# A hybrid decoder layer on one core: first norm from x loaded transposed, conditioning loads in order

## The chip, the cores and the metric

One core of a Trainium2 chip runs the whole program in one launch. The metric is the device time in microseconds (us), the median of three runs. Engines: TensorE (PE, its weight loads PEld), VectorE (DVE), ScalarE (ACT), GpSimd (POOL) and SyncE (SP), which issues most DMAs.

## The reference, cut to what matters

One step of a decoder layer over 1024 prompt rows and 8 sample rows, D_MODEL = 1024, float32. Only the beginning matters here:

```
mod = silu(c) @ w_ada + b_ada
shift1, scale1, gate1, shift2, scale2, gate2 = split(mod, 6)
h = RMSNorm(x) * (1 + scale1) + shift1
proj = h @ w_in      # conformer GLU | q, k, v | z | beta | decay | merge gates A, B
...
```

The prompt rows share one c, each of the 8 sample rows has its own. Behind proj come a Conformer branch (GLU, depthwise convolution of width 31, LayerNorm, swish, a projection), a gated DeltaNet branch (short convolution of width 4 and SiLU on q, k and v, a chunked gated delta rule with a triangular solve per chunk, a norm, a projection), the merge of the two, and a feed-forward part with its own norm; then a final norm.

## The kernel before, in words

T = 1032 columns are the 1024 + 8 rows of x. Feature-major tiles hold 128 of the 1024 features each: u[k] and the pair h_hi[k], h_lo[k], k = 0 to 7, all 128 x 1032. Products of full precision are three passes: h and each weight are split into a rounded part and the rest (h_hi and h_lo, whi and wlo), and a product is whi with h_hi, whi with h_lo, wlo with h_hi, over 344 columns each (a third of T), added up in a PSUM bank over k: 24 matmuls per bank. These are the "main products" of this text (`mm` in the profile).

hybrid() does not issue instructions. It records operations with the tiles that they read and write, and the class Plan (lines 135 to 475) orders them: a list scheduler that steps through a modelled time, keeps one queue per engine, and on each engine takes the ready operation with the lowest `plan.prio` (ties go in recorded order). Durations come from Plan.cost; tiles come out of rings with limits per class (caps: 34 slots of 4 KB and 21 of 2 KB a partition, eight PSUM banks). What it found is then emitted, so every instruction has the line of that one loop, L475, and goes by its tile's name. A change of one priority, size or dependency can thus reorder all engines, until the plans meet again.

The head of the program:
- SP loads constants, c transposed, then eight pieces of w_ada (`wk`, 256 KB each: piece q = 0) and x in nine blocks of 128 rows (`xin`, the last with the 8 sample rows). ADAQ (line 30) holds the priorities of the four conditioning pieces' loads, FIRST those of the first weights.
- Norm of x (loop at line 588): per block ACT squares and sums along the row (`ss`), POOL takes the power -1/2 (`rs`), DVE scales the rows (`xn`), TensorE transposes them (`xT`, eight 128 x 128 matmuls), ACT and DVE copy them out of PSUM into u.
- Conditioning (ada_first, line 609, called for q = 0 to 3): 32 matmuls of `wk` with cT into the bank `ada`, a copy `mo`, the transpose `adaT`, and on DVE the shift, scale and s1 = norm weight * (1 + scale) of two feature tiles.
- Per piece, for its two tiles k = 2q and 2q + 1 (line 670): DVE u[k] = u[k] * s1 + shift; ACT casts it to h_hi[k]; h_lo[k] = u[k] - h_hi[k], on DVE for even k and on POOL for odd.
- `ba`: beta and decay logits straight from u, 64 one-pass matmuls in all; from them cum (sums of the decay along a chunk), its transpose cumT, a store to DRAM (scrG) and loads of it spread over partitions (`glb`, `Gb`), which edec and Dm need.

Main products go on in an order that the plan finds: GLU columns for the Conformer (conformer, line 1113), q, k, v of one head after the other. For a head, DVE runs the short convolution (`qkvq`: one scaling and three sums of 1024 columns), ACT the SiLU, TensorE transposes (`tT`) and products of k and q (`kq`); DVE makes Dm, Am and drives the solve, half a head at a time, with small TensorE steps `i` and `j` between (32 x 32 blocks; i16, i32, j32, j64 below), then TensorE steps through the scan (`pw`, `po`, `py`, `pd`).

```
plan.prio = ADAQ[q]
wk = tl("wk", [128, 512], "wk")
SP.dma_start(wk, I["w_ada"][q, k])
...
V.tensor_scalar(uk, uk, s1[:, f, 0:1], shift[:, f, 0:1], op0=ALU.mult, op1=ALU.add)
copy(Hh[k], u[k], ("ACT",))
sub(Hl[k], u[k], f32(Hh[k]), ("DVE", "POOL")[k % 2:k % 2 + 1])
```

Of the kernel before, what the change touches and what calls it, by code (L numbers as in the profile page):

```python
# [10 lines left out]
ALU = mybir.AluOpType  # L11
# [18 lines left out]
ADAQ = (-1, 0.2, 0.4, 0.5)  # L30
# [456 lines left out]
def hybrid(tc, I, O):  # L487
    nc = tc.nc
    with ExitStack() as ctx:
        ctx.enter_context(tc.manual_schedule())  # L490

        def pool(name, space=None, st=ctx, **k):
# [14 lines left out]
            acc=("P4", 10), cs=("P4", 2), ff=("PS", 8), ada=("P4", 2),  # L507
# [71 lines left out]
        def evac_T(src, dst, i, n, cls):  # L579
            for hf in range(2):  # L580
                pb = bank(cls, "xT")
                with plan.group("PE"):
                    for k in range(4):
                        kk = 4 * hf + k
                        TE.transpose(pb[:, k * 128:k * 128 + n], src[0:n, kk * 128:(kk + 1) * 128], ident[0:n, 0:n])
                dst(hf, pb)

        for i in range(9):
            n = 128 if i < 8 else 8
            cs = slice(i * 128, i * 128 + n)  # L590
            xt = tl("xin", [128, 1024], "xin")
            SP.dma_start(xt[0:n], I["x"][i * 128:i * 128 + n])
            xn = tl("xin", [128, 1024], "xn")
            ss, rs = tl("s8", [128, 1], "ss"), tl("s8", [128, 1], "rs")
# [4 lines left out]
            def norm_T(hf, pb):  # L599
                if i == 8:  # L600
                    copy(xs[:, 4 * hf:4 * hf + 4, :], pb.rearrange("p (k c) -> p k c", c=128)[:, :, 0:8])
                    return
                pairs = [(u[4 * hf + k][:, cs], pb[:, k * 128:k * 128 + n]) for k in range(4)]
                plan.any_of({e: [(m, p, {}) for p in pairs] for e, m in (("ACT", "copy"), ("DVE", "tensor_copy"))})
            evac_T(xn, norm_T, i, n, "x")
# [3 lines left out]
        def ada_first(q):  # L609
            ps = bank("s", "ada")  # L610
            for k in range(8):
                plan.prio = ADAQ[q]
                wk = tl("wk", [128, 512], "wk")
                SP.dma_start(wk, I["w_ada"][q, k])
                wk_op[0] = plan.last
                plan.prio = -1
                if k == 0:
                    plan.touch = (ps,)
                with plan.group("PE"):
                    for j in range(4):  # L620
                        TE.matmul(ps[32 * j:32 * j + 32, 0:128], lhsT=cT[:, k, :], rhs=wk[:, j * 128:j * 128 + 128],
                                  start=(k == 0), stop=(k == 7), tile_position=(0, 32 * j))
                plan.prio = 0
# [46 lines left out]
        for q in range(4):  # L670
# [1080 lines left out]
def arrange(a):  # L1751
# [6 lines left out]
    def cols(v, n):  # L1758
# [8 lines left out]
        x=x, xT=x.T.reshape(8, 128, T).transpose(1, 0, 2), cT=c.T.reshape(8, 128, 9).transpose(1, 0, 2),  # L1767
# [59 lines left out]
```

## Time and profile before

| | us |
|---|---|
| median of three runs | 1897.24 |
| lowest, highest | 1893.27, 1898.88 |
| the profiled execution | 1896.7 |
| its span in the trace | 1895.0 |
| TensorE busy in the span | 1819.3 (96 %) |
| DVE, POOL, ACT busy | 1436.5, 856.7, 847.1 |

The profile is one execution. Times in it count from the start of the span; the profiled execution lasted 1.7 us longer than the span. The granted clock of TensorE has a mean of 0.987 of full speed over it. Idle time of TensorE, and time at a lower clock, is what the kernel can still lose; idle time of the other engines costs nothing by itself.

### The profile page before, as it was taken

What the parts mean: (1) busy time and instruction counts of PE and PEld (TensorE: products, weight loads), DVE (VectorE), ACT (ScalarE), POOL (GpSimd) and SP (SyncE); (2) the same over time, 40 slices, a digit from 0 to 9 for tenths busy, and PEclk for the clock granted to TensorE, in tenths of its full rate; (3) what the DMA queues carried; (4) which work ended last, traced back from release to release, by engine and by line L of the source; (5) the groups of instructions that cost most, each with busy time, mean ns of one, the idle gap of its engine ahead of it and who ended that gap; (6) DMA issues with size and microseconds to landing.
All of it is one profiled execution on the core that took longest, in us unless ns stands there. A gap on an engine that the chain in (4) does not pass through costs nothing. (4 is left out here: it accounts for less than half of the span.)

```text
span 1895.0 us, 41996 instructions
## 1 busy us (share of the span) xinstructions
PE 1819.3 (96%) x16205; PEld 1742.7 (92%) x16205; DVE 1436.5 (76%) x3137; ACT 847.1 (45%) x2089; POOL 856.7 (45%) x734
## 2 busy tenths in 40 slices
PE   7998999999998999999999999899999999999995
PEld 5988999989897888999999989899999999999995
DVE  6576778668788999998191767975565578999997
ACT  5444445444454545421240125555555565433344
POOL 3354445444445432543222145332322338888864
PEclk9999999999999999999999999899999999999998
DMA  9321111212122477942444754344454484553433
GB/s 344 69 73 57 65 36 41 69 35 75 60 79 75 144 248 259 341 151 80 144 164 140 226 181 165 99 146 135 138 163 132 138 265 163 167 181 126 133 124 90
DMA packets 164188, 261.46 MB, mean 138 GB/s; under 512 B 27252, under 2 KB 90876, under 8 KB 163972
## 3 DMA queue, kind: packets, MB, share of 16 engines
q1 hardware_dynamic: 158228, 241.91, 39.6%
q10 hardware_dynamic: 5760, 16.88, 2.3%
q8 instruction: 127, 2.08, 0.5%
q14 instruction: 73, 0.60, 0.1%
HBM read 189.76 MB, written 69.64 MB: 137 GB/s over the span
## 5 line engine op out<-in xcount | busy, mean ns | idle before, releaser
L475 PE MATMUL mm<-h_hi,whi 128*128 128x344 f32 x1344 | 462.0, 344 | 0.0
L475 PE MATMUL mm<-h_hi,wlo 128*128 128x344 f32 x1344 | 432.1, 321 | 3.4 <-POOL rawq L475 3.4
L475 PE MATMUL mm<-h_lo,whi 128*128 128x344 f32 x1344 | 431.6, 321 | 0.0
L475 POOL TENSOR_TENSOR wlo<-raw,whi 128x512 fp32r<-128x512 f32 x168 | 250.5, 1504 | 347.8 <-ACT whi L475 280.3
L475 PE MATMUL ff<-fbh,wp 128*128 128x258 f32 x1808 | 330.1, 283 | 3.8 <-DVE accu L475 1.7
L475 PE MATMUL ff<-bp,wp 128*128 128x258 f32 x2688 | 324.5, 283 | 1.6 <-DVE bp L475 0.9
L475 PEld LDWEIGHTS ff<-bp,wp 128*128 128x128 f32 x2688 | 323.4, 189 | 2.5 <-DVE bp L475 1.3
L475 PEld LDWEIGHTS ff<-fbh,wp 128*128 128x128 f32 x1808 | 280.5, 189 | 7.5 <-DVE accu L475 3.0
L475 PEld LDWEIGHTS mm<-h_hi,whi 128*128 128x128 f32 x1344 | 255.1, 190 | 11.4 <-issue 5.4
L475 PEld LDWEIGHTS mm<-h_hi,wlo 128*128 128x128 f32 x1344 | 254.6, 189 | 3.7 <-POOL rawq L475 3.7
L475 PE MATMUL ff<-fbl,wp 128*128 128x258 f32 x904 | 255.5, 283 | 1.7 <-DVE fbl L475 1.7
L475 PEld LDWEIGHTS mm<-h_lo,whi 128*128 128x128 f32 x1344 | 255.6, 190 | 0.0
L475 POOL TENSOR_TENSOR wp<-raw,wp 128x512 fp32r<-128x512 f32 x93 | 141.6, 1528 | 199.8 <-ACT wp L475 179.2
L475 DVE SCALAR_TENSOR_TENSOR av<-gl,vecs,av 128x1024 f32<-128x1024 f32 x120 | 181.7, 1514 | 1.9
L475 PEld LDWEIGHTS ff<-fbl,wp 128*128 128x128 f32 x904 | 170.8, 189 | 2.2 <-DVE fbl L475 2.2
L475 POOL TENSOR_TENSOR fbl<-fbl,fbh 128x516 fp32r<-128x516 f32 x100 | 149.4, 1528 | 9.8 <-issue 7.7
L475 ACT CAST wp<-raw 128x512 fp32r<-128x512 f32 x159 | 95.8, 615 | 128.6 <-DVE raw L475 54.7
L475 DVE TENSOR_TENSOR ft<-ff,ft 128x258 f32<-128x258 f32 x160 | 67.3, 422 | 92.6 <-PE ff L475 91.6
L475 ACT CAST whi<-raw 128x512 fp32r<-128x512 f32 x168 | 99.1, 619 | 79.7 <-DMA raw<-w_gdn_out 32.6
L475 ACT ACTIVATE ft<-ft 128x258 f32<-128x258 f32 x224 | 93.2, 419 | 70.9 <-DVE ft L475 66.9
L475 POOL TENSOR_TENSOR wp<-s,wp 128x512 fp32r<-128x512 f32 x31 | 53.3, 1721 | 85.3 <-ACT wp L475 85.3
L475 ACT ACTIVATE gt<-mm 128x344 f32<-128x344 f32 x72 | 32.1, 457 | 112.9 <-PE mm L475 88.1
(398 smaller groups left out, 3641.1 us busy)
## 6 DMA issues: line engine op xcount, KB each, us to landing
raw<-w_ff SPq DMA_DIRECT2D x128, 256.0 KB, 4.3
fD<-ft SPq DMA_DIRECT2D x228, 129.0 KB, 3.0
fbl<-fD SPq DMA_DIRECT2D x57, 516.0 KB, 3.5
raw<-w_in SPq DMA_DIRECT2D x112, 256.0 KB, 4.3
wk<-w_ada SPq DMA_DIRECT2D x32, 512.0 KB, 4.8
wk<-w_ada SPq DMA_DIRECT2D x32, 256.0 KB, 5.3
raw<-w_o SPq DMA_DIRECT2D x32, 256.0 KB, 4.2
sp_z<-gt ACTq DMA_DIRECT2D x8, 516.0 KB, 5.4
```

The source lines that it names most:

```text
L475: getattr(h, m)(*[x.real() if isinstance(x, Ref) else x for x in a], **{q: x.real() if isinstance(x, Ref) else x for q, x in k.items()})
```

## The change

x is no longer loaded by rows. Its transpose (made on the host already, as an input of the kernel before) is loaded straight into u[k], eight loads of 516 KB, and the 8 sample columns once more into xs. ACT squares each u[k] (1032 columns), DVE adds the squares of k = 0 to 6 up, and 18 matmuls with a single column of ones sum the two tiles (the sum and the square of k = 7) over the partitions: `ss`, nine columns. One power on POOL (128 x 9) gives rs. Two DVE products spread rs on diagonals (`dg`, four blocks of 128 x 128 each), and eight matmuls with ones make of them two PSUM banks (`rB`) that hold each prompt column's factor in all partitions; a small one does the same for the samples.

Per tile, u = u * s1 * rB is now two DVE operations of 512 columns with a bank as an operand; ACT adds the shift while it casts to h_hi (1024 columns, and 8 apart); DVE alone makes h_lo = (u + shift) - h_hi (1024, and 8 apart); ACT adds the shift to u itself, for ba.

The conditioning loads: ADAQ's first value goes from -1 to 0.05, so x is loaded ahead of w_ada. Piece 0 and the first half of piece 2 stay loads of 256 KB in the 2 KB ring; pieces 1 and 3 and the second half of piece 2 are loads of 512 KB (class wk4, up to ten slots of the 4 KB ring). TensorE's ada matmuls come in groups of 16. The Conformer's weights wait until the last conditioning load has been issued.

```diff
-ADAQ = (-1, 0.2, 0.4, 0.5)
+ADAQ = (0.05, 0.2, 0.4, 0.5)
...
-        for i in range(9):
-            n = 128 if i < 8 else 8
...
-            SP.dma_start(xt[0:n], I["x"][i * 128:i * 128 + n])
...
-            A.activation(xn[0:n], xt[0:n], AF.Square, accum_out=ss[0:n])
-            V.tensor_scalar(ss[0:n], ss[0:n], 1.0 / D, EPS, op0=ALU.mult, op1=ALU.add)
-            P.tensor_tensor(rs[0:n], ss[0:n], mhalf[0:n, 0:1], ALU.pow)
-            V.tensor_scalar(xn[0:n], xt[0:n], rs[0:n], None, op0=ALU.mult)
...
-            evac_T(xn, norm_T, i, n, "x")
+        SP.dma_start(xs, I["xT"][:, :, S:T])
+        for k in range(8):
+            SP.dma_start(u[k], I["xT"][:, k])
+            sq = tl("xin", [128, T], "sq")
+            A.activation(sq, u[k], AF.Square)
+            if k == 0:
+                sqs = sq
+            elif k < 7:
+                V.tensor_tensor(sqs, sqs, sq, ALU.add)
+        pss = bank("x", "ss")
+        with plan.group("PE"):
+            for j in range(9):
+                n = 128 if j < 8 else 8
+                for i, t in enumerate((sqs, sq)):
+                    TE.matmul(pss[0:n, j:j + 1], lhsT=t[:, j * 128:j * 128 + n], rhs=ones[:, 0:1], start=i == 0, stop=i == 1)
...
+        P.tensor_tensor(rs, ss, mhalf[:, 0:1].to_broadcast([128, 9]), ALU.pow)
...
+        for i in range(2):
+            dg = tl("xin", [128, 4, 128], "dg")
+            V.tensor_tensor(dg, ident.unsqueeze(1).to_broadcast([128, 4, 128]),
+                            rs[:, 4 * i:4 * i + 4].unsqueeze(2).to_broadcast([128, 4, 128]), ALU.mult)
+            pb = bank("x", "rB1")
+            with plan.group("PE"):
+                for j in range(4):
+                    TE.matmul(pb[:, j * 128:j * 128 + 128], lhsT=ones, rhs=dg[:, j], start=True, stop=True)
+            rB1.append(pb)
...
+                if q % 2 or (q, k4) == (2, 1):
+                    two = [tl("wk4", [128, 2, 512], "wk") for _ in range(2)]
...
+                        SP.dma_start(t, I["w_ada"][q, k:k + 2].rearrange("k p n -> p k n"))
+                else:
+                    wk = [tl("wk", [128, 512], "wk") for _ in range(4)]
...
-                uk = u[k][:, 0:S]
-                V.tensor_scalar(uk, uk, s1[:, f, 0:1], shift[:, f, 0:1], op0=ALU.mult, op1=ALU.add)
-                copy(Hh[k], u[k], ("ACT",))
-                sub(Hl[k], u[k], f32(Hh[k]), ("DVE", "POOL")[k % 2:k % 2 + 1])
+                for i in range(2):
+                    ui = u[k][:, 512 * i:512 * i + 512]
+                    V.scalar_tensor_tensor(ui, ui, s1[:, f, 0:1], rB1[i], op0=ALU.mult, op1=ALU.mult)
+                uk, us = u[k][:, 0:S], u[k][:, S:T]
+                A.copy(Hh[k][:, S:T], us)
+                A.activation(Hh[k][:, 0:S], uk, AF.Identity, bias=shift[:, f, 0:1])
+                V.tensor_tensor(Hl[k][:, S:T], us, f32(Hh[k][:, S:T]), ALU.subtract)
+                V.scalar_tensor_tensor(Hl[k][:, 0:S], uk, shift[:, f, 0:1], f32(Hh[k][:, 0:S]), op0=ALU.add, op1=ALU.subtract)
+                A.activation(uk, uk, AF.Identity, bias=shift[:, f, 0:1])
...
-            hi, lo = wload(w_in[OFF["ug"] + i], 8, (sg,))
+            hi, lo = wload(w_in[OFF["ug"] + i], 8, (sg,), after=(wk_op[0],))
...
-            hi, lo = wload(w_in[OFF["u"] + i], 8, (gl,))
+            hi, lo = wload(w_in[OFF["u"] + i], 8, (gl,), after=(wk_op[0],))
```

Since the plan is made anew, the order of the instructions changes on every engine. From TensorE's second conditioning round in mid-program on (about 750 us in the trace before; TensorE's last 8392 of 13992 matmuls) the lists are the same again, on the other engines from about half of theirs on. What moves before that is shown at three places, out of the two programs' lists of instructions (output<-inputs, shape, how many alike in a row).

The first is TensorE from its first instruction. Before, up to the second `adaT`:

```order
L475 MATMUL ada<-wk,cT 32x128 x32
L475 MATMUL adaT<-con,mo 128x128
L475 MATMUL xT<-con,xn 128x128 x48
L475 MATMUL ada<-wk,cT 32x128 x8
L475 MATMUL xT<-con,xn 128x128 x4
L475 MATMUL ada<-wk,cT 32x128 x4
L475 MATMUL xT<-con,xn 128x128 x4
...
```

And after, up to its first main product (`rB` are the two banks of factors):

```order
L475 MATMUL ss<-ones,sq 128x1 x16
L475 MATMUL ss<-ones,sq 8x1 x2
L475 MATMUL ada<-wk,cT 32x128 x32
L475 MATMUL adaT<-con,mo 128x128
L475 MATMUL rB<-dg,ones 128x128 x4
L475 MATMUL rB<-dg,ones 128x128 x4
L475 MATMUL ada<-wk,cT 32x128 x16
L475 MATMUL rB1s<-dgs,ones 128x8
L475 MATMUL ada<-wk,cT 32x128 x16
L475 MATMUL adaT<-con,mo 128x128
L475 MATMUL mm<-h_hi,whi 128x344
```

The 72 transposes are gone; 64 ada matmuls stand ahead of the first main product, and 64 behind it. Before, 84 stand ahead and 44 behind.

The second is DVE around the first head's q convolution (`st` are small sums for the norms of q and k, `glu` the Conformer's). Before, from the copy of cum on:

```order
L475 COPY gc<-cum 128x72
L475 COPY gTs<-cumT 72x128
L475 TENSOR_SCALAR egn<-egn 128x72
L475 TENSOR_TENSOR edec<-glb,gc 128x72
L475 TENSOR_SCALAR Dm<-Gb,gc 128x128 x4
L475 SCALAR_TENSOR_TENSOR glu<-sg,mm 128x344 x3
L475 TENSOR_TENSOR ktok<-tT,edec 128x512 x2
L475 TENSOR_SCALAR qkvq<-rawq,vecs 128x1024
L475 TENSOR_SCALAR st<-st 128x4
L475 SCALAR_TENSOR_TENSOR qkvq<-rawq,vecs,qkvq 128x1024
```

After, from the same copy:

```order
L475 COPY gc<-cum 128x72
L475 TENSOR_SCALAR egn<-egn 128x72
L475 COPY gTs<-cumT 72x128
L475 TENSOR_SCALAR qkvq<-rawq,vecs 128x1024
L475 TENSOR_SCALAR st<-st 128x4
L475 SCALAR_TENSOR_TENSOR qkvq<-rawq,vecs,qkvq 128x1024 x2
L475 TENSOR_TENSOR edec<-glb,gc 128x72
L475 SCALAR_TENSOR_TENSOR glu<-sg,mm 128x344
L475 TENSOR_TENSOR st<-st 128x4
L475 TENSOR_TENSOR ktok<-tT,edec 128x512
...
L475 SCALAR_TENSOR_TENSOR qkvq<-rawq,vecs,qkvq 128x1024
```

Two of qkvq's three sums have moved ahead of edec; the third stands behind it, behind Dm and both ktok. On TensorE the transposes of qkvq stand behind 291 main products after, and behind 351 before.

The third is TensorE in the solve of the second half-head (numbers of the tiles kept). Before, the last i step and the j step:

```order
L475 MATMUL i32_2210<-T32_2048,Pt_2182 32x32 x16
L475 MATMUL j32_2249<-Tt2_2242,Am_1878 32x32 x8
```

After, the same two and what stands between them:

```order
L475 MATMUL i32_1811<-T32_1676,Pt_1796 32x32 x16
L475 MATMUL mm_1830<-h_hi0_334,whi_1768 128x344
L475 MATMUL mm_1830<-h_lo0_359,whi_1768 128x344
L475 MATMUL mm_1830<-h_hi0_334,wlo_1769 128x344
L475 MATMUL pw_1834<-Sn_1809,qkvk_706 128x128
L475 MATMUL po_1836<-Sn_1809,Gb_931 128x128
...
L475 MATMUL tT_1846<-con_74,qkvv_1281 128x128 x4
...
L475 MATMUL py_1862<-R_1844,U0_78 128x128
L475 MATMUL j32_1864<-Tt2_1853,Am_1538 32x32 x8
```

Where two steps followed each other, nine main products and small ones now stand between them; from the first i step of this half-head to its j step there are 33 main products and products of the scan after, and nine before.

## Rows read from the trace of the kernel before

**Rows 1.** The page, its parts 1 and 2: busy time, share and instructions of each engine; and TensorE's busy tenths in 40 equal slices of the span.

```profile
PE 1819.3 (96%) x16205; PEld 1742.7 (92%) x16205; DVE 1436.5 (76%) x3137; ACT 847.1 (45%) x2089; POOL 856.7 (45%) x734
...
PE   7998999999998999999999999899999999999995
```

**Rows 2.** Windows of TensorE after the head: stretch, its length, busy time (instructions), granted clock, DMA share, GB/s.

```profile
60.00:100.00 40.00, 40.00 (x259) 1.00 0.46 110
100.00:200.00 100.00, 89.22 (x882) 0.93 0.16 55
200.00:400.00 200.00, 198.55 (x2074) 1.00 0.16 52
400.00:750.00 350.00, 338.62 (x4031) 0.99 0.35 120
```

**Rows 3.** TensorE's timeline: start, duration, operation, and in brackets the idle time before it and what released it.

```profile
102.05 1.09 PE L475 MATMUL tT<-con,qkvq 128*128 128x128 f32 x8 [0.88 <-ACT qkvq L475]
...
116.53 0.32 PE L475 MATMUL mm<-h_lo,whi 128*128 128x344 f32 x1
120.25 0.66 PE L475 MATMUL mm<-h_hi,wlo 128*128 128x344 f32 x1 [3.40 <-POOL rawq L475]
...
174.12 0.45 PE L475 MATMUL i<-T,Pt 32*32 32x32 f32 x32
...
179.76 0.64 PE L475 MATMUL j<-Tt,Am 32*32 32x32 f32 x16 [5.19 <-DVE Tt L475]
```

**Rows 4.** Windows of TensorE where the granted clock (the column behind the busy time) falls, and the one ahead of the first.

```profile
21.00:24.00 3.00, 1.00 (x8) 0.95 1.07 397
24.00:27.00 3.00, 3.00 (x21) 0.50 1.04 379
120.00:126.00 6.00, 5.75 (x21) 0.50 0.00 0
180.00:184.00 4.00, 4.00 (x43) 0.50 0.37 82
```

**Rows 5.** Windows of all engines in the head: length, busy time of PE, PEld, DVE, ACT, POOL, then granted clock, DMA share, GB/s.

```profile
0.00:15.00 15.00, 5.74 (x66) 1.92 (x67) 2.71 (x15) 4.52 (x8) 2.10 (x12) 1.00 0.86 303
15.00:20.00 5.00, 5.00 (x23) 4.67 (x24) 3.81 (x13) 4.69 (x15) 1.66 (x3) 1.00 1.03 409
...
35.00:46.00 11.00, 10.48 (x133) 7.59 (x128) 9.10 (x11) 3.42 (x6) 7.97 (x8) 1.00 1.05 394
```

**Rows 6.** SP's queue of DMA issues: start, time over which the loads are issued, how many.

```profile
33.82 3.90 SPq L475 DMA_DIRECT2D wk<-w_ada  x6
```

**Rows 7.** DMA issues between 36 and 37.6 us: how many, KB each, median us from issue to landing.

```profile
wk<-w_ada SPq DMA_DIRECT2D x2, 256.0 KB, 6.1
```

**Rows 8.** TensorE's timeline at its first main products.

```profile
33.71 0.42 PE L475 MATMUL ada<-wk,cT 128*32 128x128 f32 x8
...
35.15 0.42 PE L475 MATMUL mm<-h_hi,whi 128*128 128x344 f32 x1
```

**Rows 9.** A window of TensorE alone: busy time and instructions from the first main product to 60 us.

```profile
35.00:60.00 25.00, 24.48 (x249) 1.00 0.49 183
```

**Rows 10.** POOL's timeline: its first h_lo and its last.

```profile
34.97 2.48 POOL L475 TENSOR_TENSOR h_lo<-u,h_hi 128x1032 fp32r<-128x1032 f32 x1 [2.00 <-ACT h_hi L475]
...
54.48 2.50 POOL L475 TENSOR_TENSOR h_lo<-u,h_hi 128x1032 fp32r<-128x1032 f32 x1 [2.00 <-ACT h_hi L475]
```

**Rows 11.** Groups of instructions of the first 60 us: engine, operation, shapes, count, then busy us and mean ns of one, then idle time before them and its releasers.

```profile
L475 PE MATMUL xT<-con,xn 128*128 128x128 f32 x64 | 12.5, 365 | 4.6 <-DVE ss L475 2.5 <-DVE xn L475 2.0
...
L475 ACT ACTIVATE xn<-xin 128x1024 f32<-128x1024 f32 x8 | 8.5, 1077 | 0.5 <-DMA xin<-x 0.3
L475 ACT CAST h_hi<-u 128x1032 fp32r<-128x1032 f32 x8 | 8.0, 1053 | 9.8 <-POOL u L475 9.8
...
L475 DVE TENSOR_SCALAR xn<-xin,rs 128x1024 f32<-128x1024 f32 x8 | 6.7, 860 | 1.4 <-POOL rs L475 1.4
...
L475 DVE TENSOR_TENSOR h_lo<-u,h_hi 128x1032 fp32r<-128x1032 f32 x4 | 5.0, 1260 | 2.7 <-ACT h_hi L475 2.7
...
L475 POOL TENSOR_TENSOR rs<-ss,mhalf 128x1 f32<-128x1 f32 x8 | 4.4, 553 | 17.4 <-DVE ss L475 17.4
```

**Rows 12.** DVE's timeline from gTs to the end of the q convolution.

```profile
71.99 0.29 DVE L475 COPY gTs<-cumT 72x128 f32<-72x128 f32 x1 [2.41 <-PE cumT L475]
...
81.60 0.23 DVE L475 TENSOR_TENSOR edec<-glb,gc 128x72 f32<-128x72 f32 x1 [9.22 <-DMA glb<-scrG]
84.36 0.87 DVE L475 TENSOR_SCALAR Dm<-Gb,gc 128x128 f32<-128x128 f32 x4 [2.53 <-DMA Gb<-scrG]
...
87.65 0.51 DVE L475 SCALAR_TENSOR_TENSOR glu<-sg,mm 128x344 f32<-128x344 f32 x1 [1.57 <-PE mm L475]
90.54 0.69 DVE L475 TENSOR_TENSOR ktok<-tT,edec 128x512 f32<-128x512 f32 x1 [2.37 <-ACT kqs L475]
...
98.28 1.28 DVE L475 SCALAR_TENSOR_TENSOR qkvq<-rawq,vecs,qkvq 128x1024 f32<-128x1024 f32 x1
```

**Rows 13.** POOL's timeline ahead of TensorE's wait at 120 us.

```profile
115.75 2.23 POOL L475 TENSOR_TENSOR Gb<-qkvq,Gb 128x512 f32<-128x512 f32 x1
117.94 2.26 POOL L475 TENSOR_TENSOR wlo<-raw,whi 128x512 fp32r<-128x512 f32 x1
```

More of the change, by code (lines that the diff above doesn't have):

```diff
@@ L506, in hybrid @@
             g=("P4", 16), x1=("P4", 8), h2=("P4", 28), hr0=("P4", 6), hr1=("P4", 6), wc=("P4", 7), wd=("P4", 8), wo=("P4", 6), fb=("P4", 18), bp=("P2", 4),
-            acc=("P4", 10), cs=("P4", 2), ff=("PS", 8), ada=("P4", 2),
+            acc=("P4", 10), cs=("P4", 2), ff=("PS", 8), ada=("P4", 2), wk4=("P4", 10),
             raw=("P2", 9), Gb=("P2", 2), ktok=("P2", 2), vtok=("P2", 1), att=("P2", 2), Dm=("P2", 1),
@@ L578, in hybrid @@
         xs = tl("one", [128, 8, 8], "xs")
[L579 to L586, printed above, removed]
-        for i in range(9):
-            n = 128 if i < 8 else 8
-            cs = slice(i * 128, i * 128 + n)
-            xt = tl("xin", [128, 1024], "xin")
-            SP.dma_start(xt[0:n], I["x"][i * 128:i * 128 + n])
-            xn = tl("xin", [128, 1024], "xn")
-            ss, rs = tl("s8", [128, 1], "ss"), tl("s8", [128, 1], "rs")
-            A.activation(xn[0:n], xt[0:n], AF.Square, accum_out=ss[0:n])
-            V.tensor_scalar(ss[0:n], ss[0:n], 1.0 / D, EPS, op0=ALU.mult, op1=ALU.add)
-            P.tensor_tensor(rs[0:n], ss[0:n], mhalf[0:n, 0:1], ALU.pow)
-            V.tensor_scalar(xn[0:n], xt[0:n], rs[0:n], None, op0=ALU.mult)
[L599 to L604, printed above, removed]
-            evac_T(xn, norm_T, i, n, "x")
@@ new lines, in hybrid @@
+        ss, rs = tl("s8", [128, 9], "ss"), tl("s8", [128, 9], "rs")
+        V.memset(ss, 1.0)
+        V.tensor_scalar(ss[:, 0:8], pss[:, 0:8], 1.0 / D, EPS, op0=ALU.mult, op1=ALU.add)
+        V.tensor_scalar(ss[0:8, 8:9], pss[0:8, 8:9], 1.0 / D, EPS, op0=ALU.mult, op1=ALU.add)
+        P.tensor_tensor(rs, ss, mhalf[:, 0:1].to_broadcast([128, 9]), ALU.pow)
+        rB1 = []
+        dgs = tl("s8", [128, 8], "dgs")
+        for i in range(2):
[7 more added lines that the diff above has]
+            rB1.append(pb)
@@ L607, in hybrid @@
+        V.tensor_scalar(dgs, ident[:, 0:8], rs[:, 8:9], None, op0=ALU.mult)
+        pbs = bank("s", "rB1s")
+        TE.matmul(pbs[:, 0:8], lhsT=ones, rhs=dgs, start=True, stop=True)
+        V.tensor_tensor(xs, xs, pbs[:, 0:8].unsqueeze(1).to_broadcast([128, 8, 8]), ALU.mult)
         wk_op = [None]
@@ L610, in ada_first @@
             ps = bank("s", "ada")
-            for k in range(8):
+            for k4 in range(2):
                 plan.prio = ADAQ[q]
-                wk = tl("wk", [128, 512], "wk")
-                SP.dma_start(wk, I["w_ada"][q, k])
+                if q % 2 or (q, k4) == (2, 1):
+                    two = [tl("wk4", [128, 2, 512], "wk") for _ in range(2)]
+                    wk = [t[:, k] for t in two for k in range(2)]
+                    for i, t in enumerate(two):
+                        k = 4 * k4 + 2 * i
+                        SP.dma_start(t, I["w_ada"][q, k:k + 2].rearrange("k p n -> p k n"))
+                else:
+                    wk = [tl("wk", [128, 512], "wk") for _ in range(4)]
+                    for k in range(4):
+                        SP.dma_start(wk[k], I["w_ada"][q, 4 * k4 + k])
                 wk_op[0] = plan.last
                 plan.prio = -1
-                if k == 0:
+                if k4 == 0:
                     plan.touch = (ps,)
                 with plan.group("PE"):
-                    for j in range(4):
-                        TE.matmul(ps[32 * j:32 * j + 32, 0:128], lhsT=cT[:, k, :], rhs=wk[:, j * 128:j * 128 + 128],
-                                  start=(k == 0), stop=(k == 7), tile_position=(0, 32 * j))
+                    for k in range(4 * k4, 4 * k4 + 4):
+                        for j in range(4):
+                            TE.matmul(ps[32 * j:32 * j + 32, 0:128], lhsT=cT[:, k, :], rhs=wk[k % 4][:, j * 128:j * 128 + 128],
+                                      start=(k == 0), stop=(k == 7), tile_position=(0, 32 * j))
                 plan.prio = 0
```

2 lines of the change are left out of this document (1 added, 1 removed).

## The prediction

> **What bounds the kernel now.** I read the page's busy shares first: TensorE is busy 96 % of the span, and the 40 slices show its few thin places, the first slice (7), the fourth and the tenth (8) [rows 1]. So a change is worth what it takes from TensorE's idle time or its clock, and nothing else. Then the busy time by stretch [rows 2]: of 60 to 100 us nothing is idle, of 100 to 200 10.8 us, of 200 to 400 1.45, of 400 to 750 11.4. The instruction lists are the same from about 750 us on, so only the time before that can move.
>
> The 10.8 us are mainly two waits of PE's own [rows 3]: 3.40 us before 120.25 for POOL, and 5.19 before 179.76, where j waits for DVE's Tt. Behind both the granted clock is 0.50, the lower of the two levels, for some 6 and 4 us [rows 4]. A small third wait, 0.88, stands at 102.05, where the transposes of qkvq wait for ACT.
>
> The head comes last: DMA is at its full share from 15 to 46 us [rows 5], the last six conditioning loads are issued from 33.8 to 37.7 and take 6.1 us each to land, so the last of them is there at about 43.5 [rows 6, 7]. But PE takes its first main product at 35.15 [rows 8] and is then busy 24.48 of 25 us [rows 9]: from there it hardly waits for the loads, although the last h_lo is done only at 57.0 (54.48 + 2.50, [rows 10]). What counts of the head is thus when the first product can start, what small work lies behind it, and whether the pieces of h keep up.
>
> **The change, part by part.**
>
> *First product.* Away go TensorE's 72 transposes (64 of them 12.5 us busy), nine scalings (eight 6.7 us of DVE) [rows 11] and the copies into u. Now 4.2 MB of transposed x come first; at the 409 GB/s of 15 to 20 us [rows 5] that is 10.3 us, and the first issues take until about 6, so the last u is there at about 17 and the first conditioning piece (2.1 MB) at 22.5. A square takes 1.08 us [rows 11]; with the sums and 18 one-column products I come to 21.7. The power on POOL is the unknown: 0.55 us for one column [rows 11], so between 0.55 and 9 x 0.55 = 5.0 for nine; I take 2, nearer the short end, as the 0.55 holds a part that comes once: 24. Two diagonals of 128x512 at 0.69 (ktok's size, [rows 12]), the second bank of four products some 0.7 behind, two half products with a bank as operand at 0.7 (glu's 344 columns take 0.51 [rows 12], so 512 take 0.7), the cast 1.05 [rows 11]: first product at **29.2**, against 35.15: -5.95. Against it: the list has 40 more of TensorE's ada passes behind the first product (64 matmuls of two passes, was 44), at 0.42 for 8 [rows 8] +2.15; and the first h_lo comes 1.26 us after its h_hi (DVE's row [rows 11]), which PE waits out but for its first product: +1.2. **Head: -2.6** (bounds -5.95 and, with the power at 5.0, +0.4).
>
> That holds only if h keeps up. Per piece of two tiles DVE now has four half products of 0.7, two h_lo of about 1.26 and a dozen small ones, some 6.4 to 7 us, about a piece's load (2 MB at 360 to 400 GB/s: 5.5). I get h_lo at 30.5, 32, 37, 38.5, 44, 45.5, 50.6 and 52. PE, at 0.156 us a product, comes to the last two tiles at about 54 and 55.5. So the loads and DVE stay hidden, by 3 us; POOL's slow h_lo (2.5 each, [rows 10]) is gone, and ACT's extra bias pass (1.08 a tile) has room beside ACT's casts.
>
> *Clock in the head.* In the old trace 24 to 27 us ran at 0.50 although TensorE was busy all through, right behind a stretch of which it used 1 us in 3 [rows 4]. The new list has such a thin stretch before its first products. I take the same 1.5 us (half of 3.0), **+1.5**; bounds 0 and 3.0 (half of the 6 us at 120). The Trainium skill, "TensorE: Matmul & The Clock Gate", section "What's actually happening", says that the throttled state is the default and that activity releases it; by that the first products always start at the lower level, and the head would pay 3.0 rather than 1.5. The trace agrees at 24 us and not at the start, where 1.00 stands beside a TensorE that was 38 % busy [rows 5].
>
> *Transposes of qkvq.* They move from behind 351 main products to behind 291, and PE is there at about 88.9 (about 105 products are done at 60 us now, so at 57.4 with the head's -2.6; then 186 more with 18 small ones at 0.154 each, the 259 in 40 us of 60 to 100 [rows 2]). DVE's order is the one shown: gTs first, then one scaling and two of the three sums for qkvq, then edec, which comes 9.3 us behind gTs' end for the loaded glb, and Dm 2.5 more [rows 12]. The cum product stands behind 195 main products, at about 72; with cumT, for which DVE waited 2.4 [rows 12], gTs ends at about 75.4, edec comes at 84.7, Dm at 87.5; the third sum of 1.28 stands behind Dm, glu and ktok and ends at about 90.8; ACT's silu makes it 92.3. PE waits 3.5 instead of 0.9: **+2.6** (bounds 0 and, with the clock behind it, +5.5).
>
> *First stall.* PE waited at 116.85 to 120.25 for POOL's wlo, 2.26 us, which stood behind the 2.23 us of Gb [rows 13]. In the new order the second half of that weight is needed only after 517 products, and the first solve begins after 373 instead of 451; between the decay mask and the solve DVE no longer has the v convolution, and PE has 60 products, 9.4 us, over it. The wait and the half clock behind it go: 3.40 + 2.9 (half of 5.75), **-6.3** (bounds 0, if POOL is late for another weight, and -6.3).
>
> *Second stall.* Between the second solve's first i step and its j step stood 9 main products; now 33 and the products of the scan stand there. DVE's part is the same in kind, so 24 more, 3.7 us, and some 1.3 of scan products cover 5.0 of 7.2 (5.19 + half of 4): **-5.0** (bounds 0 and -7.2).
>
> *New order to 750 us.* Other pieces meet other waits. 100 to 750 us has 23.6 us of idle, 0.036 a microsecond; over 100 us that is 3.6, with the clock behind it, as above, 5.8. 200 to 400 us, in the same kind of work, has only 1.45. I take **+4.0** (0 to +5.8).
>
> *At nothing:* conditioning loads of 512 KB rather than two of 256 KB (fewer issues on SP, whose queue runs ahead of DMA; they take ten slots of the big ring, which at that time hold nothing else), conformer weights that wait for the last of them (used after 100 us), xs (0.03 MB in runs of 32 bytes; what it takes of the queue is little beside 4.2 MB, and PE at its last tiles has the 3 us above to spare).
>
> Sum: -2.6 + 1.5 + 2.6 - 6.3 - 5.0 + 4.0 = -5.8 on the profiled 1896.7: **1890.9**. The median of the three runs, 1897.24, lies 0.5 above that execution.
>
> **The rivals.**
> *B, the same, 1895.3 to 1895.9.* Either each wait costs the clock as well: +1.5 in the head and +2.9 at qkvq, -1.4 in all, 1895.3; or the second stall stays, because DVE takes other work between Tt and Am first: -0.8, 1895.9. The first of the two is what that page of the Trainium skill would make of it. For the second: DVE is busy 76 % of the span [rows 1] and its order around the solve is new. Here too falls a change that doesn't do what it says: x earlier, but h not, when the power takes 5 us.
> *C, slower, 1904.4.* The new order asks for qkvq 60 products earlier, but the chain cum, store, glb, edec and Dm runs through DMA and is not earlier by itself. If ACT is done with qkvq only at 102, as now, PE idles 13.1 instead of 0.9 us, +12.2, and the clock +2.9; with the head -1.1, the first stall -6.3 and the second still there that is +7.7. It is slower at all from a silu at 94.3 on, by over 0.3 % from 100.0. For it: DVE's waits of 9.22 and 2.53 us for these loads [rows 12] are the longest in the place. Against: two of three sums now stand ahead of the wait.
> *D, faster, 1883.2.* Both stalls go whole, and the new order has no others: -2.6 + 2.6 - 6.3 - 7.2 = -13.5, with no clock lost in the head. For it: 200 to 400 us, where the same kinds of work interleave almost without a gap.
>
> **How the numbers follow.** A measurement can tell about 0.3 %, 5.7 us: faster is below 1891.5, slower above 1902.9. Forecast 0.47 (its own range 1886 to 1896), B 0.25, C 0.13, D 0.15. Faster: two thirds of the forecast's cases and D, 0.46. The same: the other third and B, 0.41. Slower: C, 0.13. The range takes in D's end with a little over it and the forecast's bad end, not C: 1881 to 1900.
>
> **What would show it.** Right: first main product at about 29, last h_lo near 52, no main product that waits for h; a wait of 3 to 4 us at the transposes of qkvq near 89; no wait for wlo near 110 to 120; a j that waits 2 us or less; 5 us or so idle between 100 and 200 instead of 10.8. Wrong: a first product after 32; a wait at qkvq that ends after 95 (C); a j that waits 5 us (B); a granted 0.50 for over 4 us in the head (B); or idle time between 200 and 400 of more than 5 us.

## The result, and the profile after

The changed kernel takes **1919.2 us** (median of four runs, 1917.57 to 1919.44), the kernel before 1897.41 beside it: a ratio of 1.0118 (95 % interval 1.0106 to 1.0129). It is 22 us slower, where 5.8 us less were forecast, and outside the range. The profiled execution took 1919.44 us, its span 1917.7.

The page after, parts 1 and 2 (columns as in [rows 1]):

```profile
PE 1817.7 (95%) x16187; PEld 1742.3 (91%) x16187; DVE 1437.7 (75%) x3125; ACT 849.3 (44%) x2058; POOL 839.9 (44%) x720
...
PE   5989999999999999999999999899999999999995
```

TensorE is busy for about the same time in a span 22.7 us longer. The 40 slices, of 48 us each, hide where: the loss is spread thinly. The windows of [rows 2], for the changed kernel, and two behind them:

```profile
60.00:100.00 40.00, 35.98 (x238) 0.97 0.31 57
100.00:200.00 100.00, 95.04 (x978) 0.98 0.21 67
200.00:400.00 200.00, 192.59 (x2109) 1.00 0.16 51
400.00:600.00 200.00, 190.85 (x2109) 0.99 0.25 80
600.00:750.00 150.00, 141.65 (x1714) 0.97 0.41 136
750.00:900.00 150.00, 145.42 (x957) 1.00 0.65 229
```

200 to 400 us, 1.45 us idle before, has 7.4; 400 to 750 has 17.5 instead of 11.4; and 750 to 900 has 4.6, where the kernel before had none.

A better measure is how far the changed kernel lies behind at the same piece of work: the start of the n-th main product in its trace less that in the trace before (5760 in each; a sum over the `mm` records, not a row). From the 2787th product on the two lists of TensorE are the same. Ahead of it some small work lies on the other side of the n-th product; idle time and time at the lower clock, added up, give the same change as the table from the 280th to the 1000th (-3.7 us) and 14.0 us from there to the 2700th, but only 6.2 up to the 2000th. The last column is the end of the span.

| main product | 0 | 280 | 400 | 1000 | 2000 | 2700 | 3800 | end |
|---|---|---|---|---|---|---|---|---|
| before, at us | 35.2 | 89.0 | 112.3 | 272.7 | 524.9 | 741.0 | 918.5 | 1895.0 |
| after, behind by us | 2.3 | 4.4 | 13.0 | 0.7 | 12.0 | 14.3 | 22.4 | 22.7 |

The head loses 4.4 us, and 8.6 more go up to the 400th product. The stretch with the two stalls gives 12.3 back. Then 13.6 us go from the 1000th to the 2700th product (273 to 755 us), and 8.1 more up to the 3800th (941 us). From there on nothing moves.

The head of the changed kernel, TensorE's timeline (to be set beside [rows 8]), then ACT's, DVE's and POOL's:

```profile
17.17 7.14 PE L475 MATMUL ss<-ones,sq 128*128 128x1 f32 x35 [17.17 <-DVE sq L475]
...
29.55 3.41 PE L475 MATMUL rB<-dg,ones 128*128 128x128 f32 x16 [0.84 <-DVE dg L475]
...
37.33 0.33 PE L475 MATMUL adaT<-con,mo 128*128 128x128 f32 x1 [2.02 <-ACT mo L475]
37.41 0.40 PE L475 MATMUL mm<-h_hi,whi 128*128 128x344 f32 x1
...
53.74 0.33 PE L475 MATMUL adaT<-con,mo 128*128 128x128 f32 x1
```

```profile
37.01 0.26 ACT L475 COPY mo<-ada 128x128 f32<-128x128 f32 x1
```

```profile
28.09 2.01 DVE L475 TENSOR_TENSOR dg<-con,rs 128x512 f32<-128x512 f32 x2
...
54.11 0.20 DVE L475 TENSOR_TENSOR m<-adaT,vecs 128x36 f32<-128x36 f32 x1 [2.08 <-PE adaT L475]
...
58.82 1.28 DVE L475 SCALAR_TENSOR_TENSOR h_lo<-u,m,h_hi 128x1024 fp32r<-128x1024 f32 x1
```

```profile
24.67 1.80 POOL L475 TENSOR_TENSOR rs<-ss,mhalf 128x9 f32<-128x9 f32 x1 [21.12 <-DVE ss L475]
```

The first main product comes at 37.41, not earlier than 35.15, and the last h_lo ends at 60.1, not at 52 (57.0 before). TensorE's wait at the transposes of qkvq is of the size forecast, 4.02 us against 3.5. The granted clock falls to 0.50 behind it (97.3 to 104.1 us), and at the first step of the solve TensorE waits once more:

```profile
99.34 1.97 PE L475 MATMUL tT<-con,qkvq 128*128 128x128 f32 x8 [4.02 <-ACT qkvq L475]
...
118.80 0.38 PE L475 MATMUL i<-Tt,Ao 32*32 32x32 f32 x24 [1.99 <-POOL pk L475]
```

```profile
99.00:103.00 4.00, 3.65 (x15) 0.50 0.28 110
```

What TensorE waited for between 280 and 760 us (engine and tile that waited, what released it: us in total, times, longest). In the kernel before, the first four of its list:

```profile
PE pw L475 <- DVE Sn L475: 2.7, 3, 1.2
PE i L475 <- DVE Tt L475: 2.2, 1, 2.2
PE pd L475 <- DVE vn L475: 2.0, 4, 0.7
PE j L475 <- DVE Tt L475: 1.8, 1, 1.8
```

And in the changed kernel:

```profile
PE pd L475 <- DVE vn L475: 5.1, 7, 1.4
PE j L475 <- DVE Tt L475: 4.0, 3, 2.0
PE i L475 <- DVE Tt L475: 2.8, 2, 1.8
PE mm L475 <- POOL wlo L475: 2.1, 1, 2.1
PE py L475 <- DVE R L475: 2.0, 3, 0.9
```

No wait of 5 us hides the loss. It is many of 1 to 2 us, most of them at steps of the solve and of the scan that wait for DVE.

### The profile page after: what moved, and what is told of

Read it like the earlier page. It is cut to its first block, busy times and chain, and to the rows that moved or that the text cites. A ratio compares the mean times of both kernels' runs of the same rounds, so it can differ in the third digit from the quotient of the medians.

```text
span 1917.7 us, 41848 instructions
## 1 busy us (share of the span) xinstructions
PE 1817.7 (95%) x16187; PEld 1742.3 (91%) x16187; DVE 1437.7 (75%) x3125; ACT 849.3 (44%) x2058; POOL 839.9 (44%) x720
## 3 DMA queue, kind: packets, MB, share of 16 engines
q10 hardware_dynamic: 5760, 16.88, 2.3%
## 5 line engine op out<-in xcount | busy, mean ns | idle before, releaser
L475 POOL TENSOR_TENSOR wlo<-raw,whi 128x512 fp32r<-128x512 f32 x168 | 244.4, 1468 | 329.4 <-ACT whi L475 277.1
L475 DVE SCALAR_TENSOR_TENSOR av<-gl,vecs,av 128x1024 f32<-128x1024 f32 x120 | 177.0, 1475 | 1.8
L475 PE MATMUL mm<-g_hi,wlo 128*128 128x258 f32 x256 | 74.9, 292 | 4.1 <-POOL wlo L475 3.9
```

Of the source, the lines that this page charges most:

```text
L475: getattr(h, m)(*[x.real() if isinstance(x, Ref) else x for x in a], **{q: x.real() if isinstance(x, Ref) else x for q, x in k.items()})
```

## The experiments

Two theories stood against each other after this. **Theory O:** the new order of the later work costs the time. **Rival H:** the head that comes late puts the engines out of step, whatever the order. To part them, the order was taken out of the planner's hands: a table names, for each of the 10816 operations behind the head, its engine and its place in that engine's list, out of one kernel's plan, and the head's operations go in between as they become ready.

**e1 and e2: each head with the other's order.**

```diff
+MAINQ = (...)
...
+            for i, e, at in tab:
+                op, e = byidx[i + off], ("PE", "ACT", "DVE", "POOL", "SP")[e]
+                op.alts = {e: op.alts[e]}
+                rank[op] = (at, op.idx)
+                if off:
+                    line[e].append(op)
...
-                    k = x.prio
...
+                    k = rank[x]
+                    if x.idx >= self.mark and line[e][pos[e]] is not x:
+                        continue
```

Expected of e1:

> The head of the changed kernel (x transposed, one-column sums, 512 KB conditioning loads), but every engine's later work in the order of the kernel before, written out as a table; the Conformer's weights don't wait for the conditioning loads. Theory O (the new order of the later work costs it): the head's lag of 2 to 4.5 us stays and all waits after it are those of before: 1899 to 1903. Rival H (the head that starts late puts DVE, POOL and the DMA queues out of step with TensorE, and that costs the rest): 1913 to 1920, as the changed kernel. Rival of both (half and half): 1906 to 1911.

Expected of e2:

> The head of the kernel before with the later work in the order of the changed kernel, written out as a table. Theory O: the losses between 300 and 940 us are there without the new head: 1911 to 1918. Rival H: no later start, so no losses: 1895 to 1900.

Measured: e1 1904.62 (ratio 1.0045, 1.003 to 1.006), e2 1926.14 (1.0153, 1.0136 to 1.0170).

| median, us | old order | new order |
|---|---|---|
| old head | 1896.37 | 1926.14 |
| new head | 1904.62 | 1919.2 |

e1 lies 1.6 us above O's range and below both others, e2 8 above O's. e1's main products lie 6.7 us behind from the 120th to the 400th and at the 1000th, and 7.1 to 7.5 from there to the last: the late head stays a constant, and nothing is lost behind it. e2's lie 8.8 behind at the 280th, 6.1 at the 1000th, 21.7 at the 2700th and 33.0 at the 3800th: behind the 280th, the losses of the changed kernel. (The execution of e2 that was profiled is the slowest of its four, 1931.97.) TensorE's windows (length, busy, clock) of 60 to 280, 280 to 760 and 760 to 950 us show the same, in the order before, after, e1, e2:

```profile
60.00:280.00 220.00, 208.79 (x2001) 0.97 0.22 64
280.00:760.00 480.00, 467.60 (x5311) 0.99 0.32 109
760.00:950.00 190.00, 190.00 (x1209) 1.00 0.51 179
```

```profile
60.00:280.00 220.00, 209.06 (x2055) 0.98 0.20 57
280.00:760.00 480.00, 457.05 (x5178) 0.99 0.29 97
760.00:950.00 190.00, 184.27 (x1172) 1.00 0.58 205
```

```profile
280.00:760.00 480.00, 467.34 (x5340) 0.99 0.31 103
760.00:950.00 190.00, 190.00 (x1209) 1.00 0.53 187
```

```profile
280.00:760.00 480.00, 455.15 (x5198) 0.99 0.28 92
760.00:950.00 190.00, 183.93 (x1178) 0.98 0.60 214
```

Rival H is out by e1, whose head is later than the changed kernel's (6.7 us behind at the 280th product against 4.4). e2 alone wouldn't show it, as its head is late too. The two effects don't just add up: the old head is 8 us faster than the new under the old order and 7 us slower under the new. Part of that is in the heads, which aren't quite those of the two kernels, as the table changes what stands between their operations: in e2's the windows of 25 to 30 and 30 to 35 us are these:

```profile
25.00:30.00 5.00, 2.06 (x29) 0.84 1.10 352
30.00:35.00 5.00, 5.00 (x39) 0.50 1.05 363
```

TensorE is thinly used there, and then makes its transposes at the lower clock; the first main product comes at 39.03, not at 35.15. x is loaded as in the kernel before, from 5.52 us on.

**e3, e4 and e8: other orders.** In e3 (the kernel before) and e4 (the changed kernel) one number of the planner is different, in e8 three durations of the changed kernel's planner are those of the trace.

```diff
-HOP = 0.4
+HOP = 0.45
```

```diff
-                return max(n / 2400.0 + 0.0053, 0.03) / tiles
+                return max(n / 2400.0 + 0.0125, 0.03) / tiles
...
-                return max(4 * n / 2400.0, 0.13) / tiles
+                return max(4 * n / 2400.0, 0.4 if n < 16 else 0.13) / tiles
...
-            return 0.153 + n * 0.0021
+            return 0.153 + n * 0.0024
```

> The kernel before with one number of the planner changed, its allowance between engines from 0.40 to 0.45; the same operations, another order on all engines, about as far from the old one as the changed kernel's is. Theory O in its strong form (the old order is a lucky one among many, and any new order costs 5 to 20 us): 1903 to 1917. If orders are all alike and the changed kernel's loss has a cause of its own: 1894 to 1901.

> The changed kernel with the same number changed, so the new head with a third order. Theory O: somewhere between 1900 and 1925, not at the changed kernel's 1919. Rival H: the head is as late, so 1915 to 1922 again.

> The changed kernel as it is, its order made by the planner, with three durations of the planner set to what the trace shows: a main product 0.1558 instead of 0.1486 us, a one-column product 0.4 instead of 0.13, a POOL difference of 512 columns 1.38 instead of 1.23. If new orders lose because the planner's durations are off (it foresees no wait where the chip has one): 1896 to 1904. If a new order is a draw whatever the planner believes: anywhere from 1905 to 1925, as the three new orders so far (1908.7, 1915.3, 1919.2).

Measured: e3 1915.31 (1.0094, 1.0078 to 1.0110), e4 1908.71 (1.0064, 1.0045 to 1.0082), e8 **1942.37** (1.0238, 1.0218 to 1.0257). A number that means nothing for the work moves the kernel before by 19 us and the changed one by 10. That the planner's durations are a few per cent off was my explanation for it, and e8 speaks against it: with better ones the order is worse still, and outside both ranges. It is one plan of many, so the explanation isn't ruled out for other plans.

**e5, e6 and e7: which part of the head.** All three in the old order, against e1.

```diff
-            elif k < 7:
+            else:
                 V.tensor_tensor(sqs, sqs, sq, ALU.add)
...
-                for i, t in enumerate((sqs, sq)):
-                    TE.matmul(pss[0:n, j:j + 1], lhsT=t[:, j * 128:j * 128 + n], rhs=ones[:, 0:1], start=i == 0, stop=i == 1)
+                TE.matmul(pss[0:n, j:j + 1], lhsT=sqs[:, j * 128:j * 128 + n], rhs=ones[:, 0:1], start=True, stop=True)
```

> As the first experiment (new head, old order of the later work), but DVE adds up all eight squares, and TensorE sums one tile with 9 one-column products instead of two with 18. In the traces 36 passes took 7.14 us, so 18 fewer are worth 3.6 us, against one more DVE sum of 1.3 us in the same chain: 2.3 us less than the first experiment, 1901 to 1903, if the one-column products stand on the way to the first main product. If the head is held by the conditioning loads instead: 1904 to 1906, no change.

e6 has the loop over x's blocks of the kernel before and ada_first of the changed one, e7 the other way round (the diff is e7's, against the changed kernel):

```diff
-ADAQ = (0.05, 0.2, 0.4, 0.5)
+ADAQ = (-1, 0.2, 0.4, 0.5)
...
-                if q % 2 or (q, k4) == (2, 1):
...
+                wk = tl("wk", [128, 512], "wk")
+                SP.dma_start(wk, I["w_ada"][q, k])
```

> The old norm (x by rows, transposed on TensorE) with the new conditioning loads (x ahead of w_ada, 512 KB pieces, groups of 16 ada matmuls), later work in the old order. If the loads alone cost what the head costs: 1901 to 1905. If the new norm does: 1894 to 1899, as the kernel before, since x arrives 5 us earlier and its norm starts earlier.

> The new norm with the old conditioning loads (w_ada's first piece ahead of x, all in 256 KB, groups of four ada matmuls), later work in the old order. If the norm's chain (last u, sums, power, diagonals, banks) sets the first main product, x that arrives 5 us later costs 3 to 5 us on top of the first experiment: 1907 to 1910. If the loads of the later pieces set it: 1903 to 1906.

Measured: e5 1905.73 (1.0043, 1.0029 to 1.0057), e6 1895.02 (**0.9988**, 0.9979 to 0.9997), e7 1911.01 (1.0071, 1.0058 to 1.0084). The new loads are worth a little by themselves: e6's main products lie 2.0 us ahead of the old ones up to the 3800th. It is the new norm that costs, and e7, with x 5 us later, costs 5 us more than e1 (12.1 behind at the 280th product against 6.7; its time lies 1 us above the range). e5's trace has the expected 2.1 us (4.6 behind instead of 6.7), but its time doesn't, and the expectation of 1901 to 1903 was missed. In the profiled execution, the slowest of five, it isn't waits that took them. Behind the 3800th product, where e5 and e1 run the same lists, e5 loses 4.5 us and e1 0.5: the granted clock is 0.50 there for 31.2 us in e5 and for 23.4 in e1 (sums over the clock records), and half of the difference is 3.9 us. Why the clock fell more often, and what held the other four executions, is not shown.

**e9 and e10: what makes the waits.** Theory D: DVE is full of long work that isn't urgent. Rival P: TensorE's steps stand too close. Both runs keep their kernel's order and make 120 taps of the convolution on 64 columns; the other 960 are left out.

```diff
-                V.scalar_tensor_tensor(av[:, 0:S], gl[:, j:j + S], cdw[:, j, i:i + 1], av[:, 0:S],
+                V.scalar_tensor_tensor(av[:, 0:64], gl[:, j:j + 64], cdw[:, j, i:i + 1], av[:, 0:64],
```

> The changed kernel in its own order (as a table), but 120 of DVE's Conformer convolution taps (1.5 us each, 177 us in all, not urgent) work on 64 columns instead of 1024, so that they take about 0.2 us; part of the convolution is left out. Everything else and all orders stay. Theory D (the new order loses because DVE, full of such long work, comes late with the short operations that TensorE waits for): the loss behind the first 280 main products, 19 us, falls under 6, and the time lies no more than 10 us above the next kernel of this call. Rival P (the new order puts TensorE's own steps too close together, whatever DVE has beside them): the taps run in gaps, so TensorE's waits stay and the difference to the next kernel stays 17 to 23 us.

> The kernel before in its own order (as a table) with the same 120 taps on 64 columns; the same part of the convolution is left out. The measure for the run above. Few of its waits come from DVE, so 1885 to 1896 by either theory.

Measured: e9 1908.20, e10 1890.78, a difference of 17.4, just inside P's range: P, in the main. Measured against the kernel before, as the expectation had it, e9's loss behind the 280th product is 5.5 us at the 3800th, under D's 6; but e10 gains as well, and against e10, which has the same taps, it is 14.2. Between the 1000th and the 2000th product e9 loses 11.1 us against e10, the changed kernel 11.3 against the kernel before. But behind the 2700th most of the loss is gone, 2.3 us against e10 up to the 3800th instead of 8.1. There D holds. That the steps stand too close is what is left when D goes; these two runs don't test it. TensorE's waits from 760 to 950 us, of the changed kernel:

```profile
PE mm L475 <- POOL wlo L475: 3.6, 4, 1.0
PE mm L475 <- ACT whi L475: 2.0, 3, 1.1
```

and of e9:

```profile
PE mm L748 <- ACT whi L748: 1.1, 1, 1.1
PE mm L748 <- POOL wlo L748: 0.8, 1, 0.8
```

In that stretch the weights come late. What holds them is argued, not shown: SP's queue of the changed kernel waits 18.9 us for `s0b`, the sample rows' state on DVE, with weight loads (`raw`) queued behind that. In the kernel before (730 to 950 us) it waits 8.1 for `s0b`, in e9 (740 to 950) 7.2.

```profile
SPq L475 <- DVE s0b L475: 18.9, 5, 7.7
```

**e11, e12, e15, e16, e17: more room between TensorE's steps.** The planner's table MARGIN holds a step back behind what it waits for. 1.0 instead of 0.4 in e11 (changed kernel), e12 (before), e15 (e4) and e16 (e3); 0.1 in e17 (changed kernel).

```diff
-              mm=0.4, **{n: 0.4 for n in ("tT", "kq", "i16", "i32", "j32", "j64", "k64", "k64b", "k128", "pw", "py", "pd", "po")})
+              mm=0.4, **{n: 1.0 for n in ("tT", "kq", "i16", "i32", "j32", "j64", "k64", "k64b", "k128", "pw", "py", "pd", "po")})
```

> The changed kernel, its order made by the planner with one table raised: the time that TensorE's solve and scan steps (i, j, k, pw, py, pd, po, kq, tT) are held back behind the other engines' results goes from 0.4 to 1.0 us, so that more main products come between. Theory P (the new order puts TensorE's dependent steps too close behind each other for the chip): TensorE's waits between 280 and 760 us fall from 22.6 to 15 or less, and the time to 1900 to 1911. If a new order is a draw that this does not steer: 20 to 27 us of waits there, as in the four new orders so far, and 1908 to 1930.

> The kernel before with the same table raised, as the measure for the run above. Theory P: the waits between 280 and 760 us, 12.1 before, stay below 15, 1890 to 1900. If a new order is a draw: 18 us of waits or more, 1903 to 1925.

> The fourth experiment (changed kernel, allowance 0.45) with the steps held back 1.0 instead of 0.4 us. If the hold is a cause: TensorE's waits between 280 and 760 us, 19.6 there, fall to 15 or less, and the time below 1908.7 by 3 to 10. If it is a draw: 18 to 27 us and 1900 to 1925.

> The third experiment (kernel before, allowance 0.45) with the same. If the hold is a cause: the waits between 280 and 760 us, 26.3 there, fall to 15 or less, and the time from 1915.3 to 1896 to 1910. If it is a draw: 18 to 27 us and 1900 to 1925.

> The changed kernel with the steps held back 0.1 instead of 0.4 us. If the hold is a cause: more waits than the changed kernel's 22.6 between 280 and 760 us, 26 or more, and 1920 to 1935. If it is a draw: 12 to 27 us and 1897 to 1925.

Measured, with TensorE's idle time in three stretches of each trace (the sum of its gaps of over 0.1 us; each trace is one execution, the fastest of e4's, e8's and e11's, the slowest of e17's):

| kernel | held back | us | 60 to 280 | 280 to 760 | 760 to 950 |
|---|---|---|---|---|---|
| e17 (changed) | 0.1 | 1943.2 | 15.7 | 28.5 | 9.1 |
| e8 (changed) | 0.4 | 1942.4 | 8.8 | 27.3 | 1.4 |
| e3 (before) | 0.4 | 1915.3 | 5.3 | 26.3 | 3.1 |
| changed kernel | 0.4 | 1919.2 | 10.9 | 22.6 | 5.6 |
| e4 (changed) | 0.4 | 1908.7 | 8.7 | 19.6 | 0.0 |
| kernel before | 0.4 | 1896.4 (beside e1 to e4) | 10.9 | 12.1 | 0.0 |
| e16 (before) | 1.0 | 1915.2 | 7.2 | 17.6 | 8.9 |
| e12 (before) | 1.0 | 1909.3 | 5.4 | 15.0 | 13.7 |
| e15 (changed) | 1.0 | 1916.6 | 10.7 | 14.2 | 9.6 |
| e11 (changed) | 1.0 | 1895.9 | 7.3 | 11.0 | 1.9 |

The window of e17, the worst, and e11's, the best of the planner's own new orders:

```profile
280.00:760.00 480.00, 451.49 (x5155) 0.98 0.26 88
```

```profile
280.00:760.00 480.00, 468.80 (x5219) 1.00 0.33 110
760.00:950.00 190.00, 187.85 (x1351) 1.00 0.54 184
```

From 280 to 760 us the waits follow the hold: 28.5 us at 0.1, 19.6 to 27.3 in the new orders at 0.4, 11.0 to 17.6 at 1.0 (e16's 17.6 misses its 15). But part of that only leaves the window. The held-back steps come later, and in e12, e15 and e16 most of the 8.9 to 13.7 us of waits behind 760 are again at steps of the solve and scan, in e12 for example:

```profile
PE k L475 <- DVE Ut L475: 2.7, 1, 2.7
PE k64b L475 <- DVE Ut L475: 2.5, 1, 2.5
PE k L475 <- DVE U L475: 2.5, 1, 2.5
```

From 280 to 950 us the three have 23.8 to 28.7 us of waits, the new orders at 0.4 19.6 to 29.4; only e11 (12.9) and e17 (37.6) stand apart, and at 1.0 the time follows in e11 alone. So P isn't shown to be the cause: the total stays a draw. What e12 does show is a new order that loses with a head on time: 0.2 us ahead at the 280th product, 12.4 behind at the end of the span.

**e13 and e14: do head and order add up?**

> The old norm with the new conditioning loads (head of the sixth experiment, first main product 1.9 us before the old one's), and the later work in the order of the eleventh. If head and order add up: the eleventh's head lagged 2.5 us at the 280th product, this one's led by 2.0 under the old order, so 4 us less than the eleventh: 1889 to 1893. If an order only suits the head that it was made for, as the second experiment suggests: 1896 to 1904.

> The eleventh experiment's order and head, with nine one-column products instead of eighteen (all eight squares summed on DVE). If it adds up: the 2 us that the fifth experiment's trace showed in the head, 1892 to 1895. If the later waits take it up: 1895 to 1898, as the eleventh.

Their edits are those of e6 and e5, in front of the table of e11's order. Measured: e13 **1892.09** (0.9981, 0.9972 to 0.9990), e14 1897.37 (1.0002, 0.9993 to 1.0011). e13 is faster than both kernels, by 3.6 us than the one before and 26 than the changed one (by the ratios). It is as far ahead of e11, which is what adding up had forecast; in the traces it is 2.2 us ahead of e11 at the 280th product and 3.1 at the 3800th. e14's head is hardly ahead of e11's (2.2 us behind the kernel before at the 280th product, e11 2.5), and its time isn't.

## Why the prediction was wrong, step by step

| the sum's term | forecast | measured |
|---|---|---|
| head with clock | -1.1 | +4.4 (at the 280th product) |
| qkvq and the two stalls | -8.7 | -3.7 (280th to 1000th) |
| new order to 750 us | +4.0 | +13.6 (1000th to 2700th) |
| behind 750 us | 0 | +8.1 (to the 3800th) |
| to the end | 0 | +0.3 |

**The step that failed first is "New order to 750 us".** I priced it by the old order's own rate of idle time, "0 to +5.8", as though that rate were the kernel's, and over 100 of the 650 us, without a reason for the 100. It is the old order's alone: of the planner's nine new orders in the table above, eight have 14 to 29 us of waits from 280 to 760, one has 11.0, the old has 12.1. Any edit that makes the plan anew gives up the old one, and with a bound of +5.8 on that the forecast could not reach 1919. e1 and e2 show it: +15 under the new head, +30 under the old one (8.8 of it in e2's own head), and +8 for the head under the old order. Why a new order has more waits stays open: the planner's durations (e8) and steps that stand too close (e11 to e17) were tried, and neither explains the ten plans.

**"The instruction lists are the same from about 750 us on, so only the time before that can move"** was read from TensorE's list alone. DVE, ACT, POOL and SP are still in another order up to about 900 us, and TensorE, whose own list no longer differs, waits there for weights: 5.6 us in seven waits, and 8.1 of lag.

**"First product"** was forecast for 29.2 and came at 37.41. The last u was in time, and the power took 1.80 (forecast 2). The 36 passes with one column took 7.14 us, where the sum leaves at most 3.6 (21.7 less 17 and a square). The diagonals started 1.6 us behind the power, because a copy that waited for the ada passes stood ahead of them on DVE, and the first took 1.41, not 0.69. The banks took 3.41 in all, not 1.4; and the product then stood in TensorE's queue behind `adaT` of the next piece, which waited 2.02 for a copy that ACT made after both casts. **"That holds only if h keeps up"** failed in the same way, in its times: the last conditioning load was there at 42.3, but the last piece's ada passes ran at 50.53 and its adaT at 53.74, behind main products, so the last h_lo ended at 60.1. I had timed DVE's chain and the loads, but not TensorE's queue between them. It cost no wait: from 37.5 to 95 us TensorE was busy all through.

**"Clock in the head"**, +1.5 and at most 3.0, was too small a price for what the rows show, and a granted clock of 1.00 hides it. A window of the changed kernel, three pieces of its timeline, and a piece of e2's:

```profile
20.00:30.00 10.00, 8.72 (x91) 1.00 1.08 361
```

```profile
24.20 3.60 PE L475 MATMUL ada<-wk,cT 128*32 128x128 f32 x61
28.23 0.48 PE L475 MATMUL adaT<-con,mo 128*128 128x128 f32 x1 [0.43 <-DVE mo L475]
...
32.89 1.08 PE L475 MATMUL ada<-wk,cT 128*32 128x128 f32 x32
```

```profile
37.51 0.47 PE L749 MATMUL adaT<-con,mo 128*128 128x128 f32 x1
```

The trace has no clock record before 32.4 us, and 1.00 stands in the window for want of one. The instructions tell the level. The same adaT took 0.48 us at 28.23, 0.33 at 37.33, and 0.47 in e2 at 37.51, where 0.50 is recorded. Passes of 128 columns follow each other every 0.213 us up to 32.3 us (`rB`) and every 0.111 right behind it; the eight of `tT` took 1.97 us at the recorded 0.50 (99.34) and 1.09 at 1.00 [rows 3]. So TensorE ran at the lower of its two levels, 1.2 GHz, from its first work at 17.17 us to 32.4. In the kernel before it had been at work from 5.14 us on, and its passes go from 0.213 to 0.109 us at 20.3, where its clock records begin: the 1.00 of its first 15 us [rows 5], on which the prediction leans, is no reading either. The Trainium skill, "TensorE: Matmul & The Clock Gate", section "What's actually happening", has the throttled state as the default; by it the first work after 17 idle microseconds would run at the lower level. This trace agrees, by the durations above. What it cost is an estimate from these rows: at the upper level the ada passes would have taken some 2.1 us instead of 3.60 and the banks some 1.7 instead of 3.41, about 3 us of the chain to the first product; the one-column passes up to 3.6 more, if they halve as well, which no run shows.

**The stalls** were read rightly. The wait for wlo at 120 and the one of j at 180 are gone, and from the 400th to the 1000th product the changed kernel makes up 12.3 us, against the 11.3 forecast. What ate it lies ahead of that: 8.6 us, not 2.6, are lost from the 280th to the 400th product. The wait for qkvq is 3.1 us longer than before, the lower clock behind it costs about 2.4 (half of 99.34 to 104.1), and the wait for `pk` at 118.80 is 2.0. With the clock the qkvq term is 5.5, the upper bound that the prediction gave it.

**The rivals.** C had the right sign and the wrong place: the wait at qkvq ended at 99, later than its 95, but was 4.02 us and not 13.1, as TensorE came there late itself, and most of the time was lost elsewhere. B's first case, that waits cost the clock as well, held in the head and at qkvq, but its time was the old order's. None of the four was "the order as a whole is worse by more than its forecast".

## What to carry to other kernels

Where a scheduler orders a tuned program, an edit is two changes: what it does, and a new order. Price the second from the spread of a few neutral re-plans, not from the idle time of the order that was kept, and test the edit with the old order pinned: here the edit alone made +8 of +22, and taken apart it showed that one half of it (the loads) was worth having. Compare all engines' lists, not TensorE's alone, before calling a stretch unchanged.

## What the runs showed of the hardware

At the lower clock level a one-column fp32 pass with a 128 x 128 stationary tile took as long as one of 128 columns: 0.213 us from start to start, in the 32 of `ss` (17.17 us) as in the banks behind them (29.55 us, 16 in 3.41). What it takes at the upper level no run shows.

A clock of 1.00 in a window can mean that no clock record lies there. The duration of an operation that comes again, here adaT (0.48 and 0.33 us), tells the level.

A DVE product of 128 x 512 with both inputs broadcast took 0.68 us, as one with a single input broadcast does (0.69, [rows 12]). The first of the two took 1.41, with POOL at work on `wlo` beside it; in e7, where POOL did nothing beside them, both took 0.69. So the mean of 1.0 in the row above is no price of the broadcast.
